# Second branch's out-projection: four of twelve channel tiles by seven block products per pair of column tiles, and the layer norm's odd half streamed

## The chip, the cores and the metric

The kernel runs on one core of a Trainium2 chip. Its engines work side by side, each on its own instructions in order: TensorE (PE in the profile, with PEld for its weight loads), VectorE (DVE), ScalarE (ACT), GpSimd (POOL) and SyncE (SP), which here only issues DMAs. The metric is the device time of one execution in microseconds; the runs before gave 1543.89, 1544.07 and 1544.72, median 1544.07.

## The reference

One layer of a decoder trunk on 1024 positions of 1024 channels, float32:

```python
z = rms_norm(x, g_mix) @ w_in + b_in
va, ga, xb, gb, sa, sb = split(z)
u = causal_depthwise_conv(va * sigmoid(ga), conv_a_w, conv_a_b)     # width 31
y_a = silu(layer_norm(u, ln_g, ln_b)) @ w_a_out
v = rg_lru(causal_depthwise_conv(xb, conv_b_w, conv_b_b), ...)      # 1536 channels
y_b = (v * gelu(gb)) @ w_b_out                                      # 1536 -> 1024
x = x + (sigmoid(sa) * y_a + sigmoid(sb) * y_b) @ w_o
x = x + square(relu(rms_norm(x, g_mlp) @ w_1)) @ w_2
return rms_norm(x, g_final)
```

The change is in the product that gives `y_b`, and in the layer norm, which is computed during the same stage.

## The kernel before

Activations lie with channels on the partitions: a tile is 128 channels by 1024 positions, and its two halves of 512 columns hold one half of the positions each (in some stages even and odd positions). A float32 product is made of three matmuls in a faster format: an operand is split into a high part, which ACT writes as a rounded copy, and a low part, which DVE gets by subtracting the high part from the source; then high x high, high x low and low x high are added up in a PSUM bank of 128 x 512. So each operand costs one ACT copy and one DVE subtraction ("split"), and each block of 128 x 128 x 512 three matmuls.

Most stages multiply 2 x 2 blocks with seven products in place of eight, with sums and differences of the blocks on both sides. The stage z (lines 730 to 1045, `z_mm`, `z_post`) does so for the gates; its products share four banks, and ACT copies a finished partial sum from one bank into another (line 952 `z13b<-z13a`) so that several outputs can go on from it. The stage g (`gseq`, lines 1194 on) does so for the first branch's out-projection and for what follows.

The stage between them, lines 1049 to 1192 and the loop at 1651 to 1700, is the second branch's out-projection, and does not. `hg` are the twelve tiles of `v * gelu(gb)`, written to memory by z (`hgd`) and read back and split at the end of z (`hg_load`, `hg_parts`, placed by step in `ZX`, line 1009). For each of eight column tiles `j`, `b_mm(j)` issues 12 tiles x 3 passes x 2 halves = 72 matmuls into two banks (`yb`); `b_out(j - 1)` lets DVE multiply the banks of the column tile before by the gate `sb` and stores the result to `mbd`; `b_load` and `b_parts` bring and split the weights of the next ones (two pieces of 128 x 768 each).

In the same loop the layer norm over the first branch's channels runs on DVE and ACT. Its input `yd` (8 tiles) is loaded whole into `q` at j = 0 (sixteen DMAs, line 1118). `n_mean` at j = 2 gets the means by multiplying with a constant matrix on PE; `n_center` at j = 2 and 3 subtracts them, squares on ACT and adds the squares; `n_var` and `n_root` at j = 4 give the reciprocal root; `n_scale` at j = 5 multiplies by it and applies Silu on ACT. At j = 6 and 7 the operands of stage g are loaded and split. Each `o` of these functions is one half of the positions; the half with o = 1 is called odd.

The order on each engine is written out by hand: inside `tc.manual_schedule` an engine issues in program order; where instructions of one such region fall among those of another region is left to the scheduler. `at` keeps planned clocks per engine (`clk`), `later` puts DVE work on a list, `vector_work(end)` issues that list by planned readiness and then calls `fill`, which fills DVE up to `end` with taps of the convolution. Tiles come from pools of fixed size: `T` (37 tiles of 128 x 1024), `W` for weights of this stage, `EV` for half tiles (14), `bank` for the eight PSUM banks. An instruction that writes a new tile waits until the one that had its place is done with.

Of the kernel before, what the change touches and what calls it, by code (L numbers as in the profile page):

```python
# [30 lines left out]
def trunk_kernel(ctx: ExitStack, tc: tile.TileContext, x, xt_in, xt_eo, vecs, w_in, w_a_out, w_b_out,  # L31
# [407 lines left out]
    taps = {"wait": [], "now": None, "next": None, "left": 0, "hold": False}  # L439

    def fill(until):
        while clk["V"] + 0.67 <= until:
            if taps["now"] is None:
                if taps["next"] is None:
                    if not taps["wait"] or taps["hold"]:
                        return
# [533 lines left out]
    with tc.manual_schedule(engines=ENGINES):  # L980

        hg, hraw, wb0, wb0_ = [], {}, [], []

        def wb0_load(n):
            wb0_.append(T(f"wb0_{n}").rearrange("p (k c) -> p k c", c=P))
            nc.sync.dma_start(wb0_[n][:, 0:6, :], w_b_out[0, n])

        def wb0_parts(n):
            h, l = ((T)(f"wb0{x}_{n}", F32R)[:, 0:6 * P].rearrange("p (k c) -> p k c", c=P) for x in "hl")
            raw = wb0_[n][:, 0:6, :]  # L990
            nc.scalar.activation(h, raw, AF.Copy)
            later(at("A", 0.8), 0.9, nc.vector.tensor_tensor, l, raw, h.bitcast(F32), ALU.subtract)
            wb0.extend((h[:, k, :], l[:, k, :]) for k in range(6))
# [5 lines left out]

        def hg_parts(*ts):  # L1000
            for t in ts:
                h, l = ((T if t else X1)(f"hg{x}{t}", F32R) for x in "hl")
                raw = hraw.pop(t)
                nc.scalar.activation(h, raw, AF.Copy)
                later(at("A", 1.0), 1.2, nc.vector.tensor_tensor, l, raw, h.bitcast(F32), ALU.subtract)
                hg.append((h, l))

        L = len(zseq)
        ZX.update({L - 14: ((wb0_load, 0),), L - 13: ((wb0_load, 1),), L - 11: ((wb0_parts, 0),),
                   L - 10: ((wb0_parts, 1), (hg_load, 0)), L - 9: ((hg_load, 1),),  # L1010
                   L - 8: ((hg_parts, 0), (hg_load, 2)), L - 7: ((hg_parts, 1), (hg_load, 3)),
                   L - 6: ((hg_parts, 2, 3), (hg_load, 4)), L - 5: ((hg_parts, 4), (hg_load, 5, 6)),
                   L - 4: ((hg_parts, 5, 6), (hg_load, 7)), L - 3: ((hg_load, 8, 9),),
                   L - 2: ((hg_parts, 7, 8), (hg_load, 10)), L - 1: ((hg_load, 11),),
                   L: ((hg_parts, 9, 10),), L + 1: ((hg_parts, 11),)})
# [35 lines left out]
    wp = early.enter_context(tc.tile_pool(name="weights3", bufs=4, reuse_waits="tile"))  # L1051
    vp = early.enter_context(tc.tile_pool(name="evac3", bufs=14, reuse_waits="tile"))
# [3 lines left out]
    def W(name, tag, dt=F32):  # L1056
        return wp.tile([P, 6 * P], dt, tag=tag, name=name, bufs=2 if tag == "raw" else 4)
# [7 lines left out]
    braw, bw, sb, bps = {}, {0: wb0}, {}, {}  # L1065

    def b_load(j):
        for n in range(2):
            braw[j, n] = W(f"wb{j}{n}_raw", "raw").rearrange("p (k c) -> p k c", c=P)
            nc.sync.dma_start(braw[j, n], w_b_out[j, n])  # L1070

    def b_parts(j):
        bw[j] = []
        for n in range(2):
            raw = braw.pop((j, n))
            h, l = (W(f"wb{j}{n}_{x}", "w" + x, F32R).rearrange("p (k c) -> p k c", c=P) for x in "hl")
            nc.scalar.activation(h, raw, AF.Copy)
            later(at("A", 0.8), 0.92, low, l, raw, h)
            bw[j] += [(h[:, k, :], l[:, k, :]) for k in range(6)]
# [6 lines left out]
    def b_mm(j):  # L1086
        bps[j] = ps = [bank(f"yb{j}{hf}") for hf in range(2)]
        ops = [(w, wl, *hg[k]) for k, (w, wl) in enumerate(bw.pop(j))]
        if j < 7:
            todo = [x for w, wl, h, l in ops for x in ((w, h), (w, l))]  # L1090
            todo += [(wl, h) for w, wl, h, l in ops]
        else:

            todo = [x for w, wl, h, l in ops for x in ((w, h), (w, l), (wl, h))]
        for n, (a, b) in enumerate(todo):
            for hf in range(2):
                nc.tensor.matmul(ps[hf], a, b[:, HALVES[hf]], start=n == 0, stop=n == len(todo) - 1)  # L1097
        at("P", 72 * MM)

    def b_out(j):  # L1100
        ps = bps.pop(j)
        for hf in range(2):
            def mult(g, src, j, hf):
                tt(g, src.rearrange("p (n o) -> p o n", o=2), g, ALU.mult)
                nc.sync.dma_start(halved(mbd[j], hf), g)

            later(0, 0.63, mult, sb.pop((j, hf)), ps[hf], j, hf)


    q, mean, vacc, rstd = {}, {}, {}, {}  # L1110

    def n_load():
        for o in range(2):
            for kk in range(2):
                for c2 in range(2):
                    q[kk, o, c2] = a = T(f"q{kk}{o}{c2}")
                    for i in range(2):
                        nc.sync.dma_start(a[:, HALVES[i]], yd[4 * kk + 2 * c2 + i, :, HALVES[o]])

    def n_pieces(o):  # L1120
        return [(kk, c2, i) for kk in range(2) for c2 in range(2) for i in range(2)]

    def n_sum(src, name):

        h, l = (vp.tile([P, HS], F32R, tag="ev", name=name + x) for x in "hl")
        nc.scalar.activation(h, src, AF.Copy)
        ready = at("A", 0.62, clk["V"])

        def rest():
            low(l, src, h)  # L1130
            ps = nsum[name]
            nc.tensor.matmul(ps, onesm, h, start=True, stop=False)
            nc.tensor.matmul(ps, onesm, l, start=False, stop=True)
            at("P", 2 * MM)

        nsum[name] = bank(name)
        dve(0.63, ready, rest)
        return nsum[name]

    nsum = {}  # L1140

    def n_mean():
        for o in range(2):
            mean[o] = n_sum(ysum[0][:, HALVES[o]], f"mu{o}")

    def n_center(o):
        held = []

        def add(s):
            tt(vacc[o], vacc[o], s, ALU.add)  # L1150

        for kk, c2, i in n_pieces(o):
            a = q[kk, o, c2][:, HALVES[i]]
            dve(0.63, 0, tt, a, a, mean[o], ALU.subtract)
            s = EV(f"sq{o}{kk}{c2}{i}")
            if o not in vacc:
                vacc[o] = s
                nc.scalar.activation(s, a, AF.Square)
                at("A", 0.62, clk["V"])
                continue  # L1160
            nc.scalar.activation(s, a, AF.Square)
            ready = at("A", 0.62, clk["V"])
            if held:
                dve(0.63, held[0][0], add, held.pop(0)[1])
            held.append((ready, s))
        dve(0.63, held[0][0], add, held[0][1])

    def n_var(o):
        rstd[o] = n_sum(vacc[o], f"var{o}")

    def n_root(o):
        pv = rstd[o]
        v, s, r = EV(f"lv{o}"), EV(f"lsd{o}"), EV(f"lr{o}")
        nc.vector.tensor_scalar(v, pv, EPS, None, ALU.add)
        newton_rstd(r, v, s, s)
        at("V", 7.5)
        at("A", 1.9)
        rstd[o] = r

    def n_scale(kk, o):  # L1180
        for c2 in range(2):
            for i in range(2):
                a, j = q[kk, o, c2][:, HALVES[i]], 4 * kk + 2 * c2 + i
                dve(0.63, 0, tt, a, a, rstd[o], ALU.mult)
                nc.scalar.activation(a, a, AF.Silu, scale=lng_c[:, j:j + 1], bias=lnb_c[:, j:j + 1])
                at("A", 0.62, clk["V"])

# [47 lines left out]
    def g_sums(w, i, p):  # L1235
# [3 lines left out]
        if p == 7:  # L1239
            later(0, 0.63, tt, a11, a11, a21, ALU.subtract)  # L1240
            return
        s1, s2 = (W(f"gs{w}{n}_{i}", t)[:, 0:HS].rearrange("p (k c) -> p k c", c=P)
                  for n, t in ((1, "wh"), (2, "wl")))
# [367 lines left out]
    def g_get(n, f):  # L1611
# [37 lines left out]
        7: ((g_parts, "u", 5, 1), (up_lhs, 1, 5), (g_t, "u", 0, 3), (g_t, "u", 1, 3))}.items()})  # L1649
    with tc.manual_schedule(engines=ENGINES):  # L1650
        for j in range(8):
            clk["A"], clk["V"] = max(clk["A"], clk["P"] + 0.5), max(clk["V"], clk["P"] - 2)
            if j == 0:
                b_load(1)
                b_gate(0)
                n_load()
            if j == 2:
                n_mean()
            if j == 4:
                n_var(0)  # L1660
                n_var(1)
# [437 lines left out]
```

## Time and profile before

| what | value |
|---|---|
| runs, median (lowest to highest) | 1544.07 us (1543.89 to 1544.72) |
| profiled execution, span | 1542.9 us |
| instructions | 19178 |
| mean granted TensorE clock | 0.999 |
| changed stage, first yb matmul to the end of the last | 622.8 to 760.9 us |
| DMA in all | 307.82 MB, mean 200 GB/s |
| SP queue's longest wait at a weight load of this stage | 14.6 us (for DVE's wb_l) |

The profiled execution has no time of its own other than its span, which runs from its first to its last instruction; the runs' times hold what lies around the span as well. Times in the trace count from the span's start. A row such as `L1097 PE MATMUL yb<-hgh,wb_h` is line 1097 of the kernel, the engine, the operation, and the tile written and the tiles read; a matmul's length (0.39 us) is more than its distance to the next, since matmuls overlap.

### The profile page before, as it was taken

To read this page: it belongs to the slowest core of one execution; us is meant where nothing else is said; L and a number is where in the kernel's file an instruction comes from. 1 tells how busy PE (TensorE), PEld (TensorE's weight loads), DVE (VectorE), ACT (ScalarE), POOL (GpSimd) and SP (SyncE) were. 2 spreads that over 40 slices of the span, in tenths; PEclk is the share of its full clock that TensorE was granted. 3 is DMA by queue.
4 is the path that set the end of the run, shared out by engine and by line. 5 is a ranking of instruction groups with operands and counts; after the bars stand their busy time and mean duration, and the time that the engine had idled before them with its cause. 6 is when DMAs were issued, how large, how long until landed. Compare 5 with 4: busy or idle time off the path is not lost.

```text
span 1542.9 us, 19178 instructions
## 1 busy us (share of the span) xinstructions
PE 1533.1 (99%) x6782; PEld 1262.4 (82%) x6782; DVE 1222.5 (79%) x1648; ACT 903.6 (59%) x1261; POOL 184.4 (12%) x219
## 2 busy tenths in 40 slices
PE   9999999999999999999999999999999999999998
PEld 8888788888888888888888887888888888888886
DVE  6899999979899997478569879755555558888897
ACT  6648576567567667345275777554444475555553
POOL 0000000002222222000022332000000001111110
PEclk9999999999999999999999999999999999999999
DMA  8776978898997879953579898333333779888862
GB/s 347 197 189 161 251 187 222 217 280 217 247 253 196 193 191 246 327 157 116 182 201 299 197 193 204 137 122 112 113 114 111 241 216 228 223 222 224 209 130 110
DMA packets 132288, 307.82 MB, mean 200 GB/s; under 512 B 13232, under 2 KB 35248, under 8 KB 132192
## 3 DMA queue, kind: packets, MB, share of 16 engines
q1 hardware_dynamic: 101744, 230.60, 46.0%
q0 software_dynamic: 30304, 75.74, 26.9%
q8 instruction: 53, 0.87, 0.2%
q14 instruction: 43, 0.35, 0.1%
q10 hardware_dynamic: 144, 0.26, 0.0%
HBM read 147.69 MB, written 58.72 MB: 134 GB/s over the span
## 4 chain that ended last, share of the span: by engine, by line
PE 95%; DMA 2%; issue 1%; DVE 1%; SPq 0%; POOL 0%; ACT 0%; POOLq 0%; DVEq 0%
PE z L726 18%; PE d L1863 15%; PE yb L1097 8%; PE e L1983 3%; PE keep L1863 2%; PE z L258 1%; PE rg L534 1%; PE rg L536 1%; PE rg L535 1%; DMA x<-in_x_dram 1%; DMA gu<-w_raw 1%; DMA xc<-in_xt_dram 0%; PE go3f L1274 0%; PE f15d L1550 0%; PE f15c L1550 0%
## 5 line engine op out<-in xcount | busy, mean ns | idle before, releaser
L726 PE MATMUL z<-xh,win_h 128*128 128x512 f32 x400 | 124.9, 390 | 0.0
L726 PE MATMUL z<-xl,win_h 128*128 128x512 f32 x400 | 124.5, 389 | 0.0
L1875 DVE TENSOR_TENSOR acc<-acc,d 128x1024 f32<-128x1024 f32 x72 | 87.8, 1219 | 33.3 <-PE d L1863 32.6
L726 PE MATMUL z<-xh,win_l 128*128 128x512 f32 x400 | 98.2, 391 | 0.0
L726 PEld LDWEIGHTS z<-xh,win_l 128*128 128x128 f32 x400 | 75.1, 188 | 16.9
L726 PEld LDWEIGHTS z<-xh,win_h 128*128 128x128 f32 x400 | 75.0, 188 | 16.7 <-ACT win_h L67 0.7
L637 DVE SCALAR_TENSOR_TENSOR y<-u,vec,y 128x511 f32<-128x511 f32 (+14 forms) x120 | 88.3, 736 | 0.0
L726 PEld LDWEIGHTS z<-xl,win_h 128*128 128x128 f32 x400 | 75.1, 188 | 15.8
L542 ACT ACTIVATE g<-rg,vec 96x1024 f32<-96x1024 f32 x32 | 35.6, 1113 | 85.5 <-issue 46.0
L637 DVE SCALAR_TENSOR_TENSOR y<-yt,csum,y 128x511 f32<-128x511 f32 (+6 forms) x112 | 82.5, 736 | 0.0
L637 DVE SCALAR_TENSOR_TENSOR yt<-u,vec,yt 128x511 f32<-128x511 f32 (+6 forms) x112 | 82.5, 736 | 0.0
L66 POOL DMA_DIRECT2D win_l<-win_raw x25 | 21.8, 871 | 324.3 <-ACT win_l L65 312.3
L1538 ACT ACTIVATE o<-s 128x512 fp32r<-128x512 f32 x56 | 33.7, 623 | 45.7 <-DVE s L1522 26.4
L66 POOL DMA_DIRECT2D zo<-zw x42 | 36.6, 871 | 129.4 <-ACT zo L65 116.1
L1097 PE MATMUL yb<-hgl,wb_h 128*128 128x512 f32 x168 | 51.7, 389 | 0.0
L1097 PE MATMUL yb<-hgh,wb_h 128*128 128x512 f32 x168 | 51.7, 389 | 0.0
L486 DVE SCALAR_TENSOR_TENSOR v<-xb,vec,v 128x1023 f32<-128x1023 f32 (+2 forms) x36 | 46.2, 1282 | 6.9 <-ACT v L477 6.1
L66 POOL DMA_DIRECT2D db_1l<-wr x7 | 6.1, 870 | 310.5 <-ACT db_1l L65 287.9
L1097 PE MATMUL yb<-hgh,wb_l 128*128 128x512 f32 x168 | 41.0, 389 | 0.0
L65 ACT ACTIVATE zo<-zw 128x512 fp32r<-128x512 f32 x42 | 26.3, 625 | 20.7 <-PE z10f L914 2.1
L1063 DVE TENSOR_TENSOR o<-s,o 128x512 fp32r<-128x512 f32 x56 | 37.3, 683 | 0.5 <-ACT o L1538 0.5
L1097 PEld LDWEIGHTS yb<-hgh,wb_h 128*128 128x128 f32 x168 | 31.5, 188 | 6.6
(1805 smaller groups left out, 4669.7 us busy)
## 6 DMA issues: line engine op xcount, KB each, us to landing
w_raw<-in_w_dram SPq DMA_DIRECT2D x34, 512.0 KB, 5.7
fr<-fd SPq DMA_DIRECT2D x32, 512.0 KB, 6.3
wr<-in_w_dram SPq DMA_DIRECT2D x32, 512.0 KB, 6.6
zw<-in_w_in_dram SPq DMA_DIRECT2D x28, 512.0 KB, 6.3
win_raw<-in_w_in_dram SPq DMA_DIRECT2D x25, 512.0 KB, 6.8
win_l<-win_raw POOLq DMA_DIRECT2D x25, 512.0 KB, 6.7
zo<-zw POOLq DMA_DIRECT2D x42, 256.0 KB, 5.6
gates<-zg SPq DMA_DIRECT2D x32, 256.0 KB, 3.9
```

The source lines that it names most:

```text
L65: nc.scalar.activation(l, src, AF.Copy, scale=-1.0)
L66: nc.gpsimd.dma_start(l, src, accum_op=ALU.add)
L486: nc.vector.scalar_tensor_tensor(v[:, d:S], a[:, 0:S - d], cbw_c[:, w * 12 + t:w * 12 + t + 1], v[:, d:S], ALU.mult, ALU.add)
L542: nc.scalar.activation(a, gps.pop((n, gi))[:HD, :], AF.Sigmoid, bias=(ba_c, bx_c)[gi][:, n:n + 1])
L637: nc.vector.scalar_tensor_tensor(o[:, k:], a[:, 0:HS - k], c, o[:, k:], ALU.mult, add)
L726: nc.tensor.matmul(zps[s][:, HALVES[hf]], w[:, k, :], xw[k][part][hf], start=n == 0, stop=n == 23)
L1063: tt(l, src, h.bitcast(F32), ALU.subtract)
L1097: nc.tensor.matmul(ps[hf], a, b[:, HALVES[hf]], start=n == 0, stop=n == len(todo) - 1)
L1538: nc.scalar.activation(o[:, 0], src, AF.Copy)
L1863: nc.tensor.matmul(o, a, b, start=n == 0 and (p != 1 or g == 0), stop=n == len(todo) - 1, skip_group_check=p == 1 and g > 0)
L1875: tt(acc[p, q2], acc[p, q2], ps, ALU.add)
L1983: nc.tensor.matmul(o, a, b, start=n == 0 and t not in LOADED, stop=n == len(todo) - 1, skip_group_check=t in LOADED)
```

## The change

Four of the twelve channel tiles (4, 5, 10, 11, as 2 x 2 blocks with the two halves of positions) and two column tiles at a time are now multiplied by seven block products in place of eight. The other eight tiles ("plain") keep three passes per block. A step of PE is one product ("1" to "7": two channel tiles, six matmuls) or one plain block ("00", "01", "10", "11": column tile of the pair and half of the positions, 24 matmuls). `bseq` gives the order; `b_post` what follows a step: copies between banks on ACT, sums with the saved product 7 (`fs`) on DVE, the gate's multiplication. `hb_load`, `hb_t` and `hb_parts` load the four tiles' halves, form their differences and split them; `a_load`, `a_sums`, `a_parts` do so for the weights of the products, and `p_load`, `p_parts` for the plain weights. `BX` places them by step.

The layer norm becomes a generator, `n_all`, of small pieces that `n_fill` issues where DVE's planned clock has room ("pause" ends a step's filling). It does the odd half's statistics first, from pieces of 128 x 512 loaded one at a time (`n_ahead`, six of them ahead), which are centred, stored back to `yd`, and loaded again (`n_load(1)`) after the third pair; then the even half, its scaling, and the odd half's scaling. The pools become W 7 tiles of 128 x 1024, EV 15 half tiles.

```diff
-        hg, hraw, wb0, wb0_ = [], {}, [], []
+        hg, hraw, hb_, hbo, wraw_, wop = {}, {}, {}, {}, {}, {}
...
+        def hb_load(kk, hf):
+            hb_[kk, hf] = a = T(f"hb{kk}{hf}")
+            for c in range(2):
+                nc.sync.dma_start(a[:, HALVES[c]], hgd[4 + c + 6 * kk, :, HALVES[hf]])
...
+        def a_sums(i):
...
+                s1, s2, s3, s4 = (s[:, n * 2 * P:(n + 1) * 2 * P] for n in range(4))
+                for o, x, y, op_ in ((s1, a21, a22, ALU.add), (s2, s1, a11, ALU.subtract),
+                                     (s3, a11, a21, ALU.subtract), (s4, a12, s2, ALU.subtract)):
+                    later(0, 0.4, nc.vector.tensor_tensor, o, x, y, op_)
...
+        ZX.update({L - 16: ((a_load, 0),), L - 13: ((a_sums, 0), (hb_load, 0, 0)),
+                   L - 12: ((a_parts, 0, "a"), (hb_load, 0, 1)), L - 11: ((a_parts, 0, "s"), (hb_load, 1, 1)),
+                   L - 10: ((p_load, 0), (hb_load, 1, 0)), L - 9: ((hb_parts, 1),),
+                   L - 8: ((hb_t, 1, 3), (hg_load, 0)), L - 7: ((hb_t, 2), (hb_parts, 7), (hg_load, 1)),
+                   L - 6: ((hb_parts, 6), (hg_load, 2)), L - 5: ((p_parts, 0), (hg_load, 3, 6)),
+                   L - 4: ((hg_parts, 0), (hg_load, 7)), L - 3: ((hg_parts, 1), (hg_load, 8)),
+                   L - 2: ((hg_parts, 2, 3), (hg_load, 9)), L - 1: ((hb_parts, 2), (hg_parts, 6)),
+                   L: ((hg_parts, 7, 8),), L + 1: ((hg_parts, 9),)})
...
-    wp = early.enter_context(tc.tile_pool(name="weights3", bufs=4, reuse_waits="tile"))
-    vp = early.enter_context(tc.tile_pool(name="evac3", bufs=14, reuse_waits="tile"))
+    wp = early.enter_context(tc.tile_pool(name="weights3", bufs=7, reuse_waits="tile"))
+    vp = early.enter_context(tc.tile_pool(name="evac3", bufs=15, reuse_waits="tile"))
...
+    PLAIN = (0, 1, 2, 3, 6, 7, 8, 9)
+    bseq = [(0, "1")]
+    for i in range(4):
+        bseq += [(i, x) for x in ("7", "6", "00", "5", "2", "4", "01", "3", "10")]
+        bseq += [(i + 1, "1")] * (i < 3) + [(i, "11")]
...
+    def b_mm(i, x):
+        if len(x) == 1:
+            p = int(x)
+            b = {1: "b", 2: "a", 3: "e", 4: "b", 5: "e", 6: "b", 7: "f"}[p]
+            if p in (1, 7):
+                yb_[i, b] = bank(f"yb{i}{b}")
...
+            ops = [(h[:, c:c + P], l[:, c:c + P], vh[:, hs], vl[:, hs])
+                   for c, hs in ((2 * P * k0, HALVES[0]), (2 * P * k0 + P, HALVES[1]))]
...
+            b, new = {"00": "a", "01": "e", "10": "b", "11": "g"}[x], False
+            h, l = wop[2 * i + m_, "p"]
+            ops = [(h[:, n * P:(n + 1) * P], l[:, n * P:(n + 1) * P], *(a[:, HALVES[hf]] for a in hg[t]))
+                   for n, t in enumerate(PLAIN)]
...
+        todo = [y for w, wl, h, l in ops for y in ((w, h), (w, l), (wl, h))]
...
+    def b_post(i, x):
+        def copy(to, b):
+            if to == "f":
+                t = fs[i] = EV(f"ybf{i}")
+            else:
+                t = yb_[i, to] = bank(f"yb{i}{to}")
+            nc.scalar.activation(t, yb_.pop((i, b)) if to == "f" else yb_[i, b], AF.Copy)
+            at("A", 0.62)
+
+        if x in ("1", "7", "6", "5"):
+            copy(*{"1": "ab", "7": "ff", "6": "eb", "5": "ge"}[x])
+        elif x in ("2", "3"):
+            b_out(i, 0, int(x == "3"), yb_.pop((i, "a" if x == "2" else "e")))
+        elif x == "10":
+            c = EV(f"ybc{i}")
+            later(0, 0.69, tt, c, yb_.pop((i, "b")), fs[i], ALU.add)
+            b_out(i, 1, 0, c)
...
+        for n, (kk, c2, i) in enumerate(PIECES8):
+            if o:
+                n_ahead(1)
+                a = ahead.pop(0)
+            else:
+                a = q[kk, o, c2][:, HALVES[i]]
+            tt(a, a, mean[o], ALU.subtract)
+            v_at()
+            if o:
+                nc.sync.dma_start(yd[4 * kk + 2 * c2 + i, :, HALVES[1]], a)
+            s = EV(f"sq{o}{n}")
             nc.scalar.activation(s, a, AF.Square)
+            at("A", 0.62, clk["V"])
...
+    def n_fill(until):
+        while clk["V"] + 0.69 <= until and not taps["paused"]:
+            taps["paused"] = next(norm, "pause") == "pause"
...
+        BX.update({(i, "7"): ((b_gate, 2 * i), (p_parts, 2 * i + 1), (a_load, i + 1))[::1 if i else 2],
+                   (i, "6"): ((p_load, 2 * i + 2),), (i, "5"): ((a_sums, i + 1),),
+                   (i, "01"): ((a_parts, i + 1, "a"), (b_gate, 2 * i + 1)),
+                   (i, "10"): ((a_parts, i + 1, "s"), (p_parts, 2 * i + 2), (p_load, 2 * i + 3))})
+    for k, v in {(0, "1"): ((p_load, 1), (hb_parts, 5)), (0, "7"): ((hb_t, 4),), (0, "6"): ((hb_parts, 4),),
+                 (0, "00"): ((hb_parts, 3),), (0, "2"): ((p_parts, 1), (n_ahead, 6)), (0, "10"): ((n_load, 0),),
+                 (2, "11"): ((n_load, 1),),
+                 (3, "00"): ((g_load, "a", 0, 0), (g_load, "a", 1, 0)),
+                 (3, "4"): ((n_to, 4), (g_parts, "a", 1, 0), (g_parts, "a", 1, 1)),
...
+        for n, step in enumerate(bseq):
+            taps["paused"] = False
             clk["A"], clk["V"] = max(clk["A"], clk["P"] + 0.5), max(clk["V"], clk["P"] - 2)
...
+            if n:
+                b_post(*bseq[n - 1])
+            b_mm(*step)
+            for f, *a in BX.get(step, ()):
+                f(*a)
+            vector_work(clk["P"] - 0.3)
+        b_post(*bseq[-1])
```

The weights `w_b_out` arrive laid out in two arrays, `w_b_pl` for the plain tiles and `w_b_sq` for the products.

More of the change, by code (lines that the diff above doesn't have):

```diff
@@ L437, in at @@
         return clk[e] + 0.1
-    taps = {"wait": [], "now": None, "next": None, "left": 0, "hold": False}
+    taps = {"wait": [], "now": None, "next": None, "left": 0, "hold": False, "more": lambda until: None}
     def fill(until):
@@ L1063, in low @@
         tt(l, src, h.bitcast(F32), ALU.subtract)
[L1065 to L1079, printed above, removed]
+    PLAIN = (0, 1, 2, 3, 6, 7, 8, 9)
[3 more added lines that the diff above has]
+        bseq += [(i + 1, "1")] * (i < 3) + [(i, "11")]
+    sb, yb_, fs = {}, {}, {}
     def b_gate(j):
@@ L1100, in b_out @@
[L1100 to L1125, printed above, removed]
-        nc.scalar.activation(h, src, AF.Copy)
[L1127 to L1138, printed above, removed]
@@ new lines, in trunk_kernel, with n_load, v_at, n_split @@
+    q, mean, vacc, rstd, nsum, nspl = {}, {}, {}, {}, {}, {}
+    def n_load(o):
+        for kk in range(2):
+            for c2 in range(2):
+                q[kk, o, c2] = a = T(f"q{kk}{o}{c2}")
+                for i in range(2):
+                    nc.sync.dma_start(a[:, HALVES[i]], yd[4 * kk + 2 * c2 + i, :, HALVES[o]])
+    def v_at():
+        at("V", 0.69)
+    def n_split(src, name):
+        h, l = nspl[name] = [vp.tile([P, HS], F32R, tag="ev", name=name + x) for x in "hl"]
+        nc.scalar.activation(h, src, AF.Copy)
+        at("A", 0.62, clk["V"])
+        low(l, src, h)
+        v_at()
@@ new lines, in n_mm, with n_ahead @@
+    def n_mm(name):
+        h, l = nspl.pop(name)
+        nsum[name] = ps = bank(name)
+        nc.tensor.matmul(ps, onesm, h, start=True, stop=False)
+        nc.tensor.matmul(ps, onesm, l, start=False, stop=True)
+        at("P", 2 * MM)
+        return ps
+    PIECES8 = [(kk, c2, i) for kk in range(2) for c2 in range(2) for i in range(2)]
+    ahead, asked = [], [0]
+    def n_ahead(n):
+        for kk, c2, i in PIECES8[asked[0]:asked[0] + n]:
+            ahead.append(EV(f"yc{kk}{c2}{i}"))
+            nc.sync.dma_start(ahead[-1], yd[4 * kk + 2 * c2 + i, :, HALVES[1]])
+        asked[0] += n
@@ L1173, in n_root @@
+        mean.pop(o)
+        n_split(vacc.pop(o), f"var{o}")
+        yield "pause"
+        pv = n_mm(f"var{o}")
+        yield "pause"
         v, s, r = EV(f"lv{o}"), EV(f"lsd{o}"), EV(f"lr{o}")
         nc.vector.tensor_scalar(v, pv, EPS, None, ALU.add)
-        newton_rstd(r, v, s, s)
-        at("V", 7.5)
-        at("A", 1.9)
-        rstd[o] = r
[L1180 to L1186, printed above, removed]
+        nc.scalar.activation(s, v, AF.Sqrt)
@@ new lines, in n_stats, with n_scale @@
+        at("V", 0.4)
+        at("A", 1.9, clk["V"])
+        yield "pause"
+        newton_rstd(r, v, s, s, False)
+        at("V", 3.8)
+        rstd[o] = r
+        yield True
+    def n_scale(o):
+        for kk in range(2):
+            for c2 in range(2):
+                for i in range(2):
+                    a, j = q[kk, o, c2][:, HALVES[i]], 4 * kk + 2 * c2 + i
+                    tt(a, a, rstd[o], ALU.mult)
+                    v_at()
+                    nc.scalar.activation(a, a, AF.Silu, scale=lng_c[:, j:j + 1], bias=lnb_c[:, j:j + 1])
+                    at("A", 0.62, clk["V"])
+                    scaled[0] += 1
+                    yield True
+        del rstd[o]
@@ new lines, in n_all, with n_to @@
+    def n_all():
+        yield from n_stats(1)
+        while (0, 0, 0) not in q:
+            yield "pause"
+        yield from n_stats(0)
+        ysum.clear()
+        yield from n_scale(0)
+        while (0, 1, 0) not in q:
+            yield "pause"
+        yield from n_scale(1)
+    norm = n_all()
+    scaled = [0]
+    def n_fill(until):
+        while clk["V"] + 0.69 <= until and not taps["paused"]:
+            taps["paused"] = next(norm, "pause") == "pause"
+    def n_to(n):
+        while scaled[0] < n:
+            next(norm)
```

203 lines of the change are left out of this document (93 added, 110 removed).

## The prediction

> **What bounds the kernel now.** I read the totals of the page first, then its chain, then whom TensorE (PE) waited for, then the stretch of the changed stage.
>
> ```profile
> span 1542.9 us, 19178 instructions
> PE 1533.1 (99%) x6782; PEld 1262.4 (82%) x6782; DVE 1222.5 (79%) x1648; ACT 903.6 (59%) x1261; POOL 184.4 (12%) x219
> PE 95%; DMA 2%; issue 1%; DVE 1%; SPq 0%; POOL 0%; ACT 0%; POOLq 0%; DVEq 0%
> ...
> PE gu1a L1274 <- DMA gu<-w_raw: 1.7, 1, 1.7
> PE spare L345 <- POOL ones L113: 1.6, 1, 1.6
> ```
>
> PE is busy for 99% of the span, 95% of the chain is its work, and the table of waits holds two waits of PE in all, 3.3 us, both far from the change. The chain through the changed stage, by start and length:
>
> ```profile
> 614.84 2.72 PE z13a L914 x12
> ...
> 623.00 2.04 PE yb L1097 x9
> ...
> 630.48 30.60 PE yb L1097 x135
> ...
> 695.58 65.29 PE yb L1097 x288
> 760.87 2.72 PE ga0a L1274 x12
> ```
>
> These are matmuls back to back: 65.29 us / 288 = 0.2267 us each (the twelve z products in 2.72 us give the same). Nine yb matmuls ran ahead of the last two z products, so z alone would have ended at 630.48 - 2.04 = 628.4. The stage ends when its matmuls have been issued. The other engines around it (columns: PE, PEld, DVE, ACT, POOL busy with counts; clock; DMA share; GB/s):
>
> ```profile
> 361.00:600.00 239.00, 239.00 (x1056) 197.88 (x1056) 221.71 (x336) 154.54 (x264) 52.33 (x60) 1.00 0.85 213
> 600.00:640.00 40.00, 40.00 (x178) 33.14 (x177) 23.40 (x24) 29.23 (x41) 5.21 (x6) 1.00 0.97 302
> ...
> 695.00:730.00 35.00, 35.00 (x156) 28.98 (x155) 29.93 (x39) 18.31 (x25) 0.00 (x0) 1.00 0.33 106
> ...
> 622.00:761.00 139.00, 139.00 (x615) 115.06 (x614) 85.35 (x111) 55.34 (x75) 0.00 (x0) 1.00 0.58 188
> ...
> 761.00:780.00 19.00, 19.00 (x86) 15.73 (x85) 18.73 (x26) 8.77 (x15) 2.49 (x3) 1.00 0.77 235
> ```
>
> Between 622 and 761 PE is full at clock 1.00, VectorE (DVE) busy for 85.35 of 139 us, ScalarE (ACT) for 55.34, POOL not at all. One matmul less is worth 0.227 us here, as long as no copy, split or load comes late.
>
> **The change part by part.** *Matmuls.* The stage has 576 now: three groups of 168, and 72 for the first column tile.
>
> ```profile
> L1097 PE MATMUL yb<-hgh,wb_h x168: 389/389/395, 644.6 to 759.6; 128*128 128x512 f32 x168
> ...
> L1097 PE MATMUL yb<-hgl,wb_h x168: 389/389/393, 645.1 to 760.0; 128*128 128x512 f32 x168
> ...
> L1097 PE MATMUL yb<-hgh,wb_l x168: 388/389/389, 655.5 to 760.5; 128*128 128x512 f32 x168
> ```
>
> After, a pair of column tiles takes four plain blocks of 8 tiles x 3 passes (96) and seven products of 2 x 3 (42): 138 for 144, in four pairs 552 for 576. **24 x 0.2267 = 5.44 us go.** That consecutive matmuls now stay on one bank costs nothing: the z products do so already at the same 0.227. It cannot be more than 5.44 by removed waits, since PE has none in the stage.
>
> *Copies between banks, four per pair on ACT, new.* The same copy in the z stage:
>
> ```profile
> 606.29 0.39 PE L914 MATMUL z13a<-xh,zo 128*128 128x512 f32 x1
> ...
> 606.72 0.58 ACT L952 ACTIVATE z13b<-z13a 128x512 f32<-128x512 f32 x1 [1.08 <-PE z13a L914]
> ```
>
> The last matmul of z13a starts at 606.29, PE's next would at 606.52, the copy ends at 607.30: with ACT free it is done 0.78 us into PE's next step. PE's new order in a pair is 1, 7, 6, 00, 5, 2, 4, 01, 3, 10, the next pair's 1, 11, with six matmuls (1.36 us) in a product and 24 (5.44 us) in a block. So the slack is, for a to b in the first pair, 1.36 - 0.78 = **0.58 us** (later pairs have 11 in between, 6.0); for b to e 5.44 - 0.78 = 4.7; for e to g, which must be done before 01 writes e, 2.72 - 0.78 = **1.9 us**. The copy of f only frees a bank. Wholly uncovered, three copies a pair would cost 12 x 0.78 = 9.4 us; covered, nothing. I take 0.5 us, near nothing, because the z stage has the same chain and PE waited nowhere in it.
>
> *Splits and sums.*
>
> ```profile
> L1004 ACT ACTIVATE hgh<-hg x12: 1041/1061/1062, 608.4 to 634.2; 128x1024 fp32r<-128x1024 f32 x12
> L462 DVE TENSOR_TENSOR hgl<-hg,hgh x12: 1220/1225/1226, 609.5 to 635.2; 128x1024 fp32r<-128x1024 f32 x12
> ...
> L1063 DVE TENSOR_TENSOR wb_l<-wb_raw,wb_h 128x768 fp32r<-128x768 f32 x14 | 12.9, 952 | 11.8 <-ACT wb_h L1077 11.7
> ...
> L462 DVE TENSOR_TENSOR q<-q,mu 128x512 f32<-128x512 f32 x16 | 10.5, 680 | 0.0
> ...
> L1077 ACT ACTIVATE wb_h<-wb_raw 128x768 fp32r<-128x768 f32 x14 | 11.2, 834 | 22.1 <-DMA wb_raw<-in_w_b_out_dram 22.1
> ```
>
> DVE: weights, 16 lows of 1.225 for 16 of 0.952, +4.4; activations, 8 + 7 lows for 12, +3.7; four block differences of 128x1024, +4.9; eight sums with the saved f at 0.68, +5.4; sixteen weight sums of 128x256, which no row shows, between half of a 128x512 (0.34) and a whole one (0.68), I take 0.4, nearer the half: +6.4. Together +24.8 us. ACT: 16 x (1.061 - 0.834) + 3 x 1.061 + 16 copies of 0.58 = +16.1. All put into the stage, DVE has 110 and ACT 71 of 133.6 us. As sums they cost nothing; their cover is the 133.6 us of PE's own work, and without it DVE's part would cost up to 24.8. Part of it (the first pair's weights, three differences, four product splits) is done in the tail of z, where DVE has room only after 600 (221.71 of 239 busy before): the convolution's last taps end some 4 us later there, which only delays the last channel of the norm's input, not needed for another 30 us.
>
> *The layer norm.* Its statistics move from a fixed place (column tiles 2 to 5) into gaps that the planner sees on DVE, odd half first. That half is loaded in eight 256 KB pieces, centred, stored back, and loaded again at the end of the third pair: 16 DMAs more on SP's queue, 4.2 MB.
>
> ```profile
> L1118 SPq DMA_DIRECT2D q<-yd x16: 319/351/660, 637.9 to 647.7; - x16
> ...
> DMA to landing us min/median/max: 5.2/5.4/6.2
> ...
> L1185 ACT ACTIVATE q<-q,vec 128x512 f32<-128x512 f32 x16 | 11.4, 804 | 6.8 <-DVE q L462 6.8
> ...
> L1158 ACT ACTIVATE sq<-q 128x512 f32<-128x512 f32 x2 | 1.3, 632 | 8.5 <-DVE q L462 8.5
> ```
>
> Issue: 16 x 0.351 = 5.6 us of a queue that also brings weights and gates; bytes: 106 GB/s at share 0.33 is some 320 GB/s when full, so 13 us of all DMA engines, against two thirds of them idle at 695 to 730. Cover gone, 13 us; I take nothing. There is a relief too: the sixteen loads that stood in one row on SP at 637.9 to 647.7 made ACT wait 22.1 us for weights behind them. Added waits: a square waits for its subtraction, and that for its piece. Behind the square on ACT stands the copy e to g, and PE's block 01 waits for that; this is the first rival. The four mean and variance products of PE now follow one step behind their split, a chain of add, high part and low part, about 0.68 + 0.63 + 0.68 = 2.0 us by the rows of these shapes, against a step of 1.36 or 5.44: between 0 and 4 x 0.64 = 2.6 us lost, I take 0.3, since most of PE's time is in long steps.
>
> The two roots, adjacent now, get the even half's squares between them.
>
> ```profile
> L97 ACT ACT_TABLE_LOAD x1 | 1.3, 1283 | 5.4 <-DVE lv L1174 5.4
> L1185 ACT ACT_TABLE_LOAD x1 | 1.3, 1283 | 0.0
> ```
>
> Now there is one load for both roots and one for the Silu. [...] The trace cannot show whether Square needs one.
>
> **Sum.** 1542.9 - 5.44 + 0.5 + 0.3 = 1538.3 us of span. The median of the runs, 1544.07, lies 1.17 above the profiled span, so **1539.4 us**, range of this case alone 1538.3 to 1541.
>
> **The rivals.** *Slower: the streamed half holds ACT in front of the copies.* If a piece has not landed when DVE comes to it, its square and then the copy e to g are late. The price for a pair is a landing less the slack, 5.4 - 1.9 = 3.5 us; it decides from the point where ACT starts that copy more than 1.9 us after product 5. Streaming takes about two pairs and the second load falls into the fourth: 3 x 3.5 = 10.5, so 1539.4 + 10.5 = 1549.9. For it: ACT stood 8.5 us for the first subtractions of the two halves, above. Against: six pieces are asked for a product and a block, 6.8 us, ahead of use, and the filling stops 0.3 us before PE's planned end of a step. [...]
>
> *The first pair's copy a to b is late.* It has 0.58 us, and ACT takes its work in order. In front of it in the program stand the split of the last plain tile and that of product 5.
>
> ```profile
> 631.72 1.06 ACT L1004 ACTIVATE hgh<-hg 128x1024 fp32r<-128x1024 f32 x1 [1.75 <-DMA hg<-hgd]
> ```
>
> This split waited for its load; the changed kernel's last load takes about that place in SP's order. Then 631.72 + 1.06 + 1.06 + 0.58 = 634.4 for the copy, where PE wants product 6 at 628.4 + 2.72 = 631.1: 3.3 us, 1542.7. Against it: nine yb matmuls ahead of z's last products show that the order across the two stages is made by readiness, and then the copy may go first.
>
> *The norm comes late into the next stage.* DVE is full there (18.73 of 19). Its third group of products, 22 us in, needs the odd half's differences; all of the added 24.8 us pushed past the end would cost 24.8 - 22 = 3 us: 1542.4. Today's Silu ends near 728, 33 us ahead of that stage, so I think little of it. That the matmuls don't shrink is excluded by the count.
>
> **How the numbers follow.** The forecast has 0.58, the held copies 0.20, the first copy 0.17, the late norm 0.05. About 0.2% (3.1 us) is what a measurement can tell from no change: faster is under 1541.0, slower over 1547.2. The forecast gives faster 0.56, with 0.02 to no change; the two small losses fall within, bar 0.01 faster; of the held copies 0.18 is slower, 0.02 within, and 0.03 of the small losses adds to slower: **0.57, 0.22, 0.21**. The range goes from 1537.8 (all 5.44, less 0.8 for the spread of the runs, 1543.89 to 1544.72) up to 1547.5, past the small losses and two held pairs (1546.4); three held pairs are left out.
>
> **What would show it.** Right: 552 yb matmuls at 0.227, the stage from the first yb to the first product of the next some 133 us, no wait of PE above 1 us in it. The first rival shows as waits of PE in block 01 on ACT's copy, with DVE or a load of yd behind it; the second as one wait of some 3 us at the first product 6; the third as waits in the next stage's group 6. Waits of PE on a split of weights, or on gates, would be a cause I have not priced, and a first stage or z tail that ends later than 628 before the first product would make the forecast wrong too.

## The result, and the profile after

The changed kernel takes 1551.91 us (median of 5 runs, 1549.72 to 1552.56) against 1544.07 us before: ratio 1.0049, 95% interval 1.0037 to 1.0061. It is slower by 7.8 us where 4.7 us of gain were forecast, and it lies above the predicted range. The profiled execution ran for 1549.72 us, the fastest of the five. Its totals, its chain by engine, and the table of whom TensorE waited for (columns: us in total, times, longest):

```profile
span 1548.0 us, 19213 instructions
PE 1530.0 (99%) x6758; PEld 1258.2 (81%) x6758; DVE 1247.2 (81%) x1679; ACT 917.4 (59%) x1280; POOL 184.4 (12%) x219
PE 89%; issue 4%; DMA 2%; DVE 1%; POOL 1%; ACT 1%; SPq 0%; POOLq 0%; ACTq 0%; DVEq 0%
...
PE yb0b L1141 <- ACT yb0a L1161: 4.5, 1, 4.5
PE yb3e L1141 <- ACT yb3e L1161: 2.3, 1, 2.3
...
PE mu L1202 <- DVE mu0l L1101: 0.8, 1, 0.8
```

PE has its 24 matmuls less, and a busy sum that is only 3.1 us smaller; three waits stand in a stage that had none, 7.5 us. The largest is the first pair's copy a to b (in the code it writes `yb0a` from `yb0b`). ACT's order of time around it (start, length, line, what it writes and reads, in brackets the idle time before and what ended it):

```profile
630.08 1.05 ACT L991 ACTIVATE hg8h<-hg 128x1024 fp32r<-128x1024 f32 x1
632.88 1.06 ACT L991 ACTIVATE hg9h<-hg 128x1024 fp32r<-128x1024 f32 x1 [1.75 <-DMA hg<-hgd]
633.85 0.74 ACT L937 ACTIVATE zg<-zu,vec 128x512 f32<-128x512 f32 x1
634.50 1.04 ACT L991 ACTIVATE hb5h<-hb 128x1024 fp32r<-128x1024 f32 x1
635.44 0.57 ACT L1161 ACTIVATE yb0a<-yb0b 128x512 f32<-128x512 f32 x1
```

The copy stands fifth. Its source was finished with product 1, whose six matmuls end by 630.3; from then on it waited for a split whose tile had not landed (`hg9`), a gate of the z stage and the split for product 5. PE meanwhile:

```profile
631.22 0.39 PE L1141 MATMUL yb0f<-hb7h,wbs0l 128*128 128x512 f32 x1
636.07 0.50 PE L1141 MATMUL yb0b<-hb6h,wbs0h 128*128 128x512 f32 x1 [4.46 <-ACT yb0a L1161]
```

What follows the gap is seen only in the granted clock (stretch, length, PE, PEld, DVE, ACT and POOL busy with counts, clock, DMA share, GB/s):

```profile
636.00:640.00 4.00, 3.93 (x11) 3.12 (x12) 2.82 (x3) 2.51 (x5) 0.00 (x0) 0.61 0.86 248
640.00:645.00 5.00, 5.00 (x23) 4.11 (x22) 3.08 (x6) 0.54 (x1) 0.00 (x0) 0.97 0.99 343
```

and in the lengths of two groups of the chain of waits:

```profile
636.07 2.26 PE yb0b L1141 x6
638.33 6.44 PE yb0a L1141 x24
```

PE counts as full there, but at a clock of 0.61 it issues 11 matmuls in 4 us: 30 matmuls take 8.70 us where 30 x 0.2267 is 6.80, **1.9 us more**. Of this 0.3 stands behind a wait that leaves the clock at 1.00 as well (7.10 us for the same 30 matmuls in the second experiment below), so 1.6 us are the slow clock's.

The second wait is the copy b to e of the last pair. Rows of SP, DVE and ACT in front of it:

```profile
724.47 6.50 SPq L1151 DMA_DIRECT2D mbd<-sb  x2
731.06 4.15 SPq L1185 DMA_DIRECT2D q<-yd  x8
...
729.69 0.69 DVE L1150 TENSOR_TENSOR sb<-ybc,sb 128x512 f32<-128x512 f32 x1
735.36 5.57 DVE L1268 TENSOR_TENSOR q<-q,lr 128x512 f32<-128x512 f32 x8 [4.97 <-DMA q<-yd]
...
736.09 5.84 ACT L1270 ACTIVATE q<-q,vec 128x512 f32<-128x512 f32 x8 [5.70 <-DVE q L1268]
741.84 1.04 ACT L991 ACTIVATE wbp7h<-wbp 128x1024 fp32r<-128x1024 f32 x1
742.79 0.57 ACT L1161 ACTIVATE ybf<-yb3f 128x512 f32<-128x512 f32 x1
743.26 0.58 ACT L1161 ACTIVATE yb3e<-yb3b 128x512 f32<-128x512 f32 x1
```

The odd half's second load was issued when SP came past a store that waited for DVE's multiplication at 729.69; DVE then stood 4.97 us for the first piece, ACT 5.70 us for DVE, and eight Silus, a split and a copy stand before the copy that PE wants. The third wait is the mean's low part, behind a reciprocal and a weight split on DVE.

The stage runs from 628.72 us (first yb) to 765.95 us (first product of the next): 137.23 us. Of these 560 matmuls (552 and the norm's eight) at 0.2267 take 126.95, the three waits 7.5, the 30 matmuls behind the first wait 1.9, and 0.9 is left in pieces too small for the table of waits. The stage before took 132.47 us (628.4 to 760.87). From its end to the end of the span both kernels take the same: 1548.0 - 765.95 = 782.05 and 1542.9 - 760.87 = 782.03. So the traced execution loses 5.1 us, 4.8 of them by the length of the stage and 0.3 because it starts later; what the median loses beyond that is taken up as open below.

### The profile page after: what moved, and what is told of

It is laid out like the page before. It is cut to its first block, busy times and chain, and to the rows that moved or that the text cites. A ratio compares the mean times of both kernels' runs of the same rounds, so it can differ in the third digit from the quotient of the medians.

```text
span 1548.0 us, 19213 instructions
## 1 busy us (share of the span) xinstructions
PE 1530.0 (99%) x6758; PEld 1258.2 (81%) x6758; DVE 1247.2 (81%) x1679; ACT 917.4 (59%) x1280; POOL 184.4 (12%) x219
## 4 chain that ended last, share of the span: by engine, by line
PE 89%; issue 4%; DMA 2%; DVE 1%; POOL 1%; ACT 1%; SPq 0%; POOLq 0%; ACTq 0%; DVEq 0%
PE z L726 18%; PE d L1948 15%; PE e L2068 3%; PE keep L1948 2%; PE z L258 1%; PE rg L536 1%; PE rg L534 1%; PE rg L535 1%; DMA x<-in_x_dram 1%; PE yb0b L1141 1%; ACT q L1270 1%; POOL go L66 1%; PE yb3e L1141 1%; PE yb1b L1141 1%; PE yb0e L1141 1%
## 5 line engine op out<-in xcount | busy, mean ns | idle before, releaser
L66 POOL DMA_DIRECT2D zo<-zs x28 | 24.5, 873 | 76.2 <-ACT zo L65 70.9
L578 DVE TENSOR_TENSOR_SCAN g<-a,g 128x1024 f32<-128x1024 f32 x12 | 27.5, 2292 | 0.4
L66 POOL DMA_DIRECT2D ga<-gsa x8 | 7.0, 871 | 170.4 <-ACT ga L65 168.3
L67 ACT ACTIVATE win_h<-win_raw 128x1024 fp32r<-128x1024 f32 x25 | 26.2, 1046 | 0.0
```

The costliest lines, as they stand in the source:

```text
L66: nc.gpsimd.dma_start(l, src, accum_op=ALU.add)
L578: nc.vector.tensor_tensor_scan(i, a, i, 0.0, ALU.mult, ALU.add)
```

## The experiments

My theory after the trace: the loss is the two late copies and the clock behind the first, each copy held only by what stands before it in its queue; without them the change gives what was forecast. Rivals: that another wait takes the place of a removed one; that DVE's added 24.7 us make the stage DVE-bound, so that fewer matmuls could bring nothing; and, for the clock, that the place and not the gap's length lowers it. The first four kernels shared 22 runs of the kernel before (median 1544.11), the next three 27 (1544.31), the last two 8 (1543.59).

### One split out of the way

```diff
-(0, "1"): ((p_load, 1), (hb_parts, 5)), (0, "7"): ((hb_t, 4),), (0, "6"): ((hb_parts, 4),),
+(0, "1"): ((p_load, 1),), (0, "7"): ((hb_t, 4),), (0, "6"): ((hb_parts, 5), (hb_parts, 4)),
```

> Edit: in the first pair, the split of product 5's operand goes behind the copies a to b and f, everything else as in the changed kernel. Theory (ACT's order holds the copy: ahead of it stand the last plain tile's split, which waits for its load until 632.9, a sigmoid, and this split of 0.95 us): PE's wait before the first product 6 falls by the length of the split, from 4.46 to about 3.5 us, no more, because the load still comes first. The clock of 0.61 right behind that wait costs 1.7 us in the changed kernel; if the clock falls for gaps longer than something between 3.5 and 4.5 us it goes too, and the time falls by 2.7 instead of 1.0. Rival (PE waits for something else, such as the load itself through another operand): no change.

Measured: 1551.58 us (1550.28 to 1552.21, 5 runs), ratio 1.0047 (1.0034 to 1.0059). The wait did shrink by the split's length, but the time fell by only 0.3 us by the medians, where 1.0 was expected:

```profile
PE yb0b L1141 <- ACT yb0a L1161: 3.4, 1, 3.4
...
634.98 2.93 PE yb0b L1141 x6
637.90 7.06 PE yb0a L1141 x24
```

The same 30 matmuls take 9.99 us, 3.2 above full clock where it was 1.9. The wait's cause is confirmed; in this trace the microsecond went into a longer stretch of slow clock. (The profiled span, 1550.4 us, is even 2.4 us longer than before the edit; 1.7 of that lie behind the stage, 1550.4 - 766.67 = 783.73 us against 782.05, where nothing was edited.)

### The first pair's copy in front

The split of `hg9` goes behind the copy as well:

```diff
-                   L: ((hg_parts, 7, 8),), L + 1: ((hg_parts, 9),)})
+                   L: ((hg_parts, 7, 8),)})
...
+(0, "1"): ((p_load, 1),), (0, "7"): ((hg_parts, 9), (hb_t, 4)), (0, "6"): ((hb_parts, 5), (hb_parts, 4)),
```

> Edit: the split of the last plain tile (tile 9) goes behind the copy a to b, and the split of product 5's operand behind the copy of f. Theory: the copy runs some 0.2 us after product 1, PE's 4.46 us wait and the low clock behind it (1.7 us) both go, and tile 9 is split by 635.2, before PE wants it in block 00 (637.6): the time falls by about 6 us against the changed kernel, to some 1546 by the median. Rival (the loads at the change of stage are late as such): the wait only moves to tile 9 in block 00 or to product 5, and the time falls by less than 3 us.

Measured: 1546.61 us (1544.9 to 1547.65, 11 runs), ratio 1.0015 (1.0006 to 1.0024), profiled span 1543.1. The chain and the waits:

```profile
631.72 0.49 ACT yb0a L1161
...
632.26 1.66 PE yb0b L1141 x6
633.92 5.44 PE yb0a L1141 x24
...
PE yb3e L1141 <- ACT yb3e L1161: 2.7, 1, 2.7
PE yb0b L1141 <- ACT yb0a L1161: 1.0, 1, 1.0
```

The block behind the copy is back at 5.44 us, no wait for tile 9 appears, and 5.3 us are gone by the medians, where about 6 were expected. By the trace it is 3.5 of this wait and 1.6 of clock (8.70 - 7.10), less 0.4 by which the second wait grew: 4.7, as the stage's length has it (132.57 us, 628.37 to 760.94, against 137.23). The rival's wait at another place did not come. The traced execution is the fastest of the eleven: four ran at a mean granted clock of 0.999 (1544.90 to 1546.36 us), seven at 0.997 or 0.998 (1546.10 to 1547.65).

### The odd half's scaling later

The scaling that waits for the second load may start only from block 00 of the last pair on, so that it stands behind the copy that it held (`odd_ok` is filled at step (3, "00")):

```diff
-        while (0, 1, 0) not in q:
+        while not odd_ok:
             yield "pause"
         yield from n_scale(1)
```

> Edit: the odd half's scaling may only be filled in from block 00 of the last pair on, two products later than in the changed kernel. Theory: in the last pair ACT reaches the copy b to e ahead of the eight Silus that wait for the second load of the odd half; PE's wait of 2.3 us before product 5 of the last pair goes, with 0.3 us of slow matmuls behind it, about -2.6 us against the changed kernel; nothing is lost at the end, since stage g wants the odd half only in its third group. Rival (the norm is too much work for DVE and ACT at the end): the wait moves to the copy e to g, to product 3 or into stage g, and the time stays within 1 us.

Measured: 1548.74 us (1548.01 to 1550.28, 6 runs), ratio 1.0031 (1.0019 to 1.0042). ACT's rows at the last pair:

```profile
737.38 0.58 ACT L1161 ACTIVATE yb3e<-yb3b 128x512 f32<-128x512 f32 x1 [0.76 <-PE yb3b L1141]
737.88 5.75 ACT L1270 ACTIVATE q<-q,vec 128x512 f32<-128x512 f32 x8
```

Now ACT waits for PE at the copy, and the same eight Silus run without a break behind it. The wait at `yb3e` is gone (-3.2 us by the medians, where 2.6 were expected). The profiled span fell by 1.1 us only, since in this execution the first pair's wait was 5.5 us in place of 4.5:

```profile
637.19 2.93 PE yb0b L1141 x6
640.12 5.84 PE yb0a L1141 x24
```

### Both

> Edit: both of the last two. Theory: the two waits are independent, so the gains add, about -8.6 us: from the changed kernel's profiled span of 1548.0 to 1539.4, where the kernel before has 1542.9. What then remains of the loss is the wait of 0.8 us for the mean and small ones. Rival: the saved matmuls do not become time because the next stage is held by DVE or DMA anyway; then the span stops near the 1542.9 of the kernel before.

Measured: 1542.28 us (1541.63 to 1545.93, 11 runs), ratio 0.999 (0.9981 to 0.9998); profiled span 1540.5. By medians it is 9.6 us under the changed kernel, against 5.3 + 3.2 = 8.5 one by one; by the profiled spans it is 7.5, where 8.6 were expected, since 0.9 us of the first pair's wait are left. The span lies below the 1542.9 of the kernel before, so the rival that the next stage holds the time up fails too. The same kernel measured once more, beside the next two:

> The kernel with both copies mended, once more, to share a chip and its runs of the kernel before with the two below: again about 1542.3 us, ratio 0.999, waits of PE in the stage 0.9 us (yb0b) and 0.8 us (mu).

1543.42 us (1542.21 to 1544.04, 11 runs), ratio 0.9991 (0.9982 to 1.0), span 1541.1, and the waits 0.9 and 0.8 as named.

### The last two waits

On top of both edits a second pause before the mean's products, and the first pair's remaining splits in this order:

```diff
-L - 1: ((hb_parts, 2), (hg_parts, 6)),
+L - 1: ((hg_parts, 6),),
...
+(0, "7"): ((hg_parts, 9), (hb_parts, 2)), (0, "6"): ((hb_t, 4), (hb_parts, 5)),
+(0, "00"): ((hb_parts, 4), (hb_parts, 3)),
...
         yield "pause"
+        yield "pause"
         mean[o] = n_mm(f"mu{o}")
```

> Both copies mended, and besides the mean's products one pause later and the splits of the differences for product 4, tile 5 and product 2 moved behind the copies of the first pair. My theory (what is left of the loss is the last two waits, 0.9 and 0.8 us): both go, the profiled span falls by about 1.7 us from 1540.5 to some 1538.8, the median to about 1540.6. The rival (each split that is put back is missed by a product further on): a new wait of 1 to 3 us at product 6, 5 or 2 or in block 00 of the first pair, and no gain, 1542 to 1544.

Measured: 1541.57 us (1540.76 to 1543.02, 11 runs), ratio 0.9984 (0.9975 to 0.9993): 2.7 us under the runs of the kernel before, the best version here. The mean's wait went, the copy's fell to 0.3 us, and no new wait stands in the stage, which is now full (the table of waits, and the stretch of the stage):

```profile
PE z13e L914 <- DMA zo<-zs: 0.8, 1, 0.8
PE yb0b L1141 <- ACT yb0a L1161: 0.3, 1, 0.3
```

```profile
629.00:757.00 128.00, 127.68 (x563) 105.30 (x562) 100.42 (x131) 64.55 (x87) 0.00 (x0) 1.00 0.63 207
```

It takes 127.83 us (629.48 to 757.31), 4.6 less than before the change. By the medians it is 1.85 us under the run with both edits beside it. The profiled span fell by only 0.7, to 1540.4: the stage is 1.7 us shorter (127.83 against 129.50), but it starts 0.3 us later, after a wait for a load at the end of z (`z13e`, above; 0.2 us in the other run), and what follows the stage took 0.6 us longer.

### Matmuls put back

Product 7 is issued twice in each pair, the second time into a bank begun anew, so that only PE's time changes, and with it the time that the first pair's copy has (1.36 us more):

> Both copies mended, and product 7 of each pair issued twice into its bank, the second time starting it anew: 24 matmuls more, the same result. If the stage is set by PE's matmuls at 0.2267 us, as the prediction's main term has it, this gives the 5.44 us back, less up to 0.9 us of the first pair's wait for the copy, which gets 1.36 us more: 1542.3 + 4.5 to 5.4 = 1546.8 to 1547.7. If the stage is set by DVE or by ACT's copies instead, the extra matmuls lie in their shadow and the time rises by less than 2 us.

Measured: 1545.82 us (1544.78 to 1547.09, 11 runs), ratio 1.001 (1.0002 to 1.0019): 2.4 us above the run that shared its chip, under my 4.5 to 5.4 and just above the rival's 2. The trace tells why:

```profile
629.00:761.00 132.00, 132.00 (x584) 109.21 (x583) 99.19 (x131) 63.67 (x87) 0.00 (x0) 1.00 0.61 200
```

The 584 matmuls of the stage fill it without a gap: 132.65 us (628.86 to 761.51), 0.2271 each. So the stage is PE's, and DVE (99.19 of 132) is not its bound. My figure was too high because both waits went, not one, and some of the restarts with them: the stage rose by 132.65 - 129.50 = 3.15 us. The other 0.7 us of the difference lies outside the stage and is within what the same kernel gave on two occasions (1542.28 and 1543.42 above).

### What lowers the clock

In the traces so far gaps of 3.4, 4.5 and 5.5 us lowered it (mean granted clock 0.74 from 632 to 645 us, 0.61 from 636 to 640, 0.79 from 632 to 648) and those of 2.3 and 2.7 did not (1.00 from 743 to 748 and from 738 to 745), but the first three all stood in the first pair and the others in the last. So the kernel with the first copy mended got its last pair's copy b to e twice, and five times (4 in place of the 1):

```diff
+            for _ in range(1 if (i, to) == (3, "e") else 0):
+                nc.scalar.activation(t, yb_[i, b], AF.Copy)
             nc.scalar.activation(t, yb_.pop((i, b)) if to == "f" else yb_[i, b], AF.Copy)
```

> The kernel with the first pair's copy mended (its wait at the last pair's copy b to e was 2.7 us and left the clock at 1.00), with that copy b to e issued twice in the last pair: 0.5 us more of wait, about 3.2 us, no other work changed. If the length of TensorE's gap decides whether its clock falls, and the border lies at 3.4 us or just under, the clock stays at 1.00 behind this wait and the time rises by 0.5 us alone. If the border lies between 2.7 and 3.2 us, the clock falls and the time rises by 2.4 to 3.7 us (0.5 and the 1.9 to 3.2 us that the slow matmuls cost behind the other gaps).

> The same with that copy issued five times: 4 x 0.52 = 2.1 us more of wait, about 4.8 us. If the gap's length decides, the clock falls to some 0.6 behind it, as it did behind the gaps of 3.4 to 5.5 us in the first pair, and the time rises by 2.1 + 1.9 to 3.2 = 4.0 to 5.3 us over the kernel with the first pair's copy mended (1546.6). If the place decides (the first pair lies behind the z stage and the last pair does not), the clock stays at 1.00 and it rises by 2.1 us.

Measured: 1548.14 us (1547.09 to 1550.58, 5 runs), ratio 1.0032 (1.0019 to 1.0046), and 1551.46 us (1549.98 to 1552.56, 4 runs), ratio 1.0049 (1.0033 to 1.0066). The 18 matmuls behind the wait, in the chains with one, two and five copies:

```profile
738.86 1.66 PE yb3e L1141 x6
740.52 1.38 PE yb3a L1141 x6
741.90 1.36 PE yb3b L1141 x6
```

```profile
739.35 2.54 PE yb3e L1141 x6
741.90 2.06 PE yb3a L1141 x6
743.96 1.39 PE yb3b L1141 x6
```

```profile
741.28 2.93 PE yb3e L1141 x6
744.21 2.56 PE yb3a L1141 x6
746.77 1.56 PE yb3b L1141 x6
```

and PE's last matmul before the wait and the first behind it, with one copy and with two:

```profile
735.79 0.39 PE L1141 MATMUL yb3a<-hg9h,wbp6l 128*128 128x512 f32 x1
738.86 0.50 PE L1141 MATMUL yb3e<-hb5h,wbs3h 128*128 128x512 f32 x1 [2.69 <-ACT yb3e L1161]
```

```profile
735.78 0.39 PE L1141 MATMUL yb3a<-hg9h,wbp6l 128*128 128x512 f32 x1
739.35 0.50 PE L1141 MATMUL yb3e<-hb5h,wbs3h 128*128 128x512 f32 x1 [3.18 <-ACT yb3e L1163]
```

The waits are 2.7, 3.2 and 4.7 us; the 18 matmuls take 4.40, 5.99 and 7.05 us, and the granted clock from 742 to 744 us is 0.69 with two copies and 0.50 with five, where it is 1.00 from 740 to 744 with one. The stage ends at 760.94, 763.02 and 766.01. So in these traces the length decides and not the place: half a microsecond of wait more, from 2.7 to 3.2 (from start to start of those matmuls 3.07 and 3.57), made the stage 0.5 + 1.6 = 2.1 us longer, and five copies made it 5.1 us longer. My figures were for the whole time. By the medians it rose by 1.5 us (2.05 if each is set against its own runs of the kernel before), above the 0.5 of a border at 3.4 us (the shortest gap that had lowered the clock before) but below the 2.4 that I gave as the least, and by 4.85 (5.4) with five copies, against 4.0 to 5.3. A reason for the smaller rise may be that the gap of some 2.7 us lowers the clock in some executions of the kernel with one copy, whose mean clock was 0.997 or 0.998 in seven of eleven; they have no trace. Each length was traced once, that of 2.7 us twice, so the border is a border of these executions.

## Why the prediction was wrong, point by point

*Matmuls, -5.44.* Right: 24 are gone, they run at 0.2267 us, and the stage is PE's wherever nothing holds it. The check in the prediction's last part, a stage of some 133 us, holds the tail of z as well: 133.6 is 139 - 5.44, from the window that begins at 622, while z alone would have ended at 628.4. Counted from there its own terms give 132.47 - 5.44 + 0.8 = 127.8. That the stage with all waits mended took 127.83 is so near by luck: it has 0.3 us of one wait and 0.6 of small pieces over its matmuls, not the 0.5 and 0.3 of the forecast.

*Copies between banks, +0.5.* **This is the step that failed.** They cost 4.46 + 2.27 us of waits and 1.9 us behind the first of them, 1.6 of it the slow clock, together 8.6 us. The ground given, that z has the same chain without a wait, holds only where ACT is free when the copy comes; neither copy met that.

*The rival "the first pair's copy a to b is late".* It came, at the place named and with the two splits named in front. It was argued away by the nine yb matmuls that ran ahead of z's last products in the old trace. That showed freedom for PE's work there; it showed nothing of ACT, whose copy (635.44) stayed behind the split of `hg9` (632.88). Its price was 1.2 us short in the wait: the tile landed later (the split started at 632.88, not 631.72), the z stage's gate of 0.74 us was left out; against that, PE got there 0.3 us later. The clock behind it was not in the sum. In the traces it fell behind waits of 3.2 us and more and not behind those of 2.7 and less (counted from start to start of the matmuls 3.57 and 3.07 us), and a stop that lowered it cost 1.6 to 2.9 us besides its own length.

*The rival "the streamed half holds ACT in front of the copies".* Its mechanism came once, in another place: not in the first pairs, where six pieces asked ahead sufficed and PE waited for none of them, but at the second load, whose eight pieces were issued late behind a store on SP. And it held copy b to e, not e to g, for 2.27 us instead of 3 x 3.5. The prediction counted SP's sixteen issues (5.6 us) and their bytes, and took nothing for them; what it did not follow was what stood in front of them on SP. That the store made the loads late is read from the trace; the runs moved the Silus, not the store.

*Splits and sums.* DVE +24.7 busy (24.8 worked out), ACT +13.8 (16.1), and as sums they cost nothing. The weight sums, for which 0.4 us was taken:

```profile
L462 DVE TENSOR_TENSOR wbs<-wba 128x256 f32<-128x256 f32 x6 | 2.5, 421 | 3.5 <-DMA wba<-in_w_b_sq_dram 3.5
```

*The norm's products, +0.3.* 0.8, at the first mean only. *The roots.* The even half's squares between the two roots brought no further table load:

```profile
L1254 ACT ACT_TABLE_LOAD x1 | 1.3, 1283 | 0.6 <-DVE lv L1253 0.6
L1270 ACT ACT_TABLE_LOAD x1 | 1.3, 1283 | 0.0
```

It is one load of 1.28 us for both roots and one for the Silu, as before. *The norm late in the next stage.* It did not come: 782.05 us against 782.03 behind the stage.

*Span and runs.* The 1.17 us added to the span compared it with the median of other runs; the profiled execution's own time exceeds its span by 1.72 here. That alone set the forecast some 0.6 us low. The rest adds up: 8.1 us more for the copies than forecast, 0.5 for the norm's products, 0.9 in small pieces and a start 0.3 later make 9.8 us, where the profiled span lies 9.7 above the 1538.3 of the sum.

*Open:* the four other runs of the changed kernel are 1.7 to 2.8 us longer than the profiled one, at a mean granted clock of 0.996 to 0.997 against 0.998. 0.001 of 1548 us is 1.5 us, so longer slow stretches would account for it. The first experiment's traced execution, at 0.996, has such a stretch (2.9 us lost in place of 1.6), but also 1.7 us more behind the stage; the four runs have no trace, and it is not shown.

## What to carry to other kernels

A copy that the bottleneck waited for was late here by everything that stood before it in its engine's order, the tail of the former stage included (two splits and a gate on ACT, for a wait of 4.46 us); list that order, and do not trust to readiness because another engine's work moved. A bulk load put behind stores was issued here only when the stores' data were ready (SP was at the stores from 724.47 to 730.97 us, and at the eight loads from 731.06), so the work that needs it is best issued behind whatever the bottleneck needs next, as eight Silus moved behind one copy showed (3.2 us by the medians). And a gap of TensorE of 3.2 to 5.5 us cost 1.6 to 2.9 us here besides its own length, so shortening one from 4.5 to 3.4 us brought only 0.3 us by the medians, while half a microsecond between 2.7 and 3.2 us changed the stage by 2.1.

## What the runs showed of the hardware that was not expected

The cost behind a gap does not grow evenly with it. A gap of 2.7 us left the clock at 1.00. Against the same matmuls behind a short gap at full clock (7.10 us for 30, 4.40 for 18), 3.2 us cost 1.6 more, 3.4 us 2.9, 4.5 us 1.6, 4.7 us 2.7 and 5.5 us 1.7 (8.77 - 7.10), each in one execution. In the changed kernel the fall came only after the restart (the first matmul at 636.07, the spacing of 0.43 us in place of 0.227 from 636.87 on):

```profile
636.63 0.41 PE L1141 MATMUL yb0b<-hb6h,wbs0l 128*128 128x512 f32 x1
636.87 0.60 PE L1141 MATMUL yb0b<-hb6h,wbs0h 128*128 128x512 f32 x1
637.27 0.63 PE L1141 MATMUL yb0b<-hb6l,wbs0h 128*128 128x512 f32 x1
```

What sets the size of the cost, and when behind a gap the clock falls, no run here shows.
